# Routing order fixed by hand and low weights last in three-part products, in a hybrid S5, SSD and PEER encoder layer

## The chip, the cores and the metric

The kernel runs on one core of one Trainium2 chip. The metric is the device time of one execution in microseconds. The engines are called PE (TensorE, matmuls), DVE (VectorE), ACT (ScalarE), POOL (GpSimd) and SP (SyncE, which here issues DMAs). PEld is PE's loading of weights.

## The reference

One layer on 512 tokens of width 1024: RMS norm, one input projection, a bidirectional S5 scan, a bidirectional SSD (a convolution and chunked state space), an output projection, and a PEER feed-forward, with residuals around both halves. All is float32; the kernel does its large products in three parts, with each operand split into a high and a low half. What matters here is the feed-forward:

```
q = (x2 @ w_q) as 8 heads x 2 sides x 128
scores = q . sub_keys               # 128 keys a side
s, i = top 16 of each side          # per token, head, side
cand = s[0][:, None] + s[1][None]   # 256 sums, top 16 of these
gate = softmax(best 16);  expert = i0 * 128 + i1   # 16384 experts
y = sum_over_experts gate * gelu(x2 . u[expert]) * v[expert]
```

## The kernel before

The layer is one instruction stream per engine. The order within each stream is set by a scheduler that models costs and follows priorities; the kernel's text gives the dependences. The front (norms, projections, S5, SSD) fills the first 670 us; the feed-forward then has these parts.

*Scores* (`route_scores`): 16 products with `w_q`, 16 small products with the sub-keys, and top16 on DVE by repeated MAX8, FIND_INDEX8 and MATCH_REPLACE8 (`top16`).

*Pick* (`route_pick(t)`, one for each of four tiles of 128 tokens): DVE adds the candidates (`cand`, L954), takes the top 16 per head, turns positions into index pairs (`ge`, `oha`, `ohm`, `ij`, L986 to L998) and normalizes the gates (Exp on ACT, L966; L1003 on DVE). For t of 1 to 3, PE transposes `ij` (L1016, two) and the gates (L1018), and ACT copies the latter (`kS`, L1020).

*Gathered* (`gathered`): token tile 0 is done by indirect DMAs that POOL issues (L1130), with the products on DVE. It needs only the pick of t = 0.

*Gates* (`gates(t)`, t of 1 to 3): 16 pairs of onehots each. DVE makes three tiles a pair (L1035, L1040, L1044), ACT four slices (L1039), PE eight matmuls (L1058, two groups of four), ACT copies to `stg` (L1060), and SP writes `stg` to `G_d` in DRAM (L1062). So the gate of every expert and token stands in `G_d`.

*Dense* (`up(i)` and `dense`): token tiles 1 to 3 are computed against all 128 blocks i of 128 experts. `up(i)` loads a tile of u (`wload`: `w_raw` by DMA, cast to `w_hi` on ACT, `w_lo` as the difference, on POOL for i under NF = 34 and on DVE after), makes 24 matmuls into `hid` (`mm3`, 8 steps of three) and applies Gelu into F (34 buffers). `hid` has two buffers, `w_hi` and `w_lo` two, `w_raw` three. Then for each i, `dense` loads v, multiplies F by its slice of G (L1101; a load G8 serves eight i and reads all of `G_d`), splits the product into Wh and Wl, and accumulates 18 matmuls into six banks (L1113 to L1115); afterwards `up(i + 34)`.

So `up(0)` to `up(33)` need no routing and are what PE can do while the routing runs on DVE; the accumulation needs all 24 writes of `G_d`. The scheduler decides between which tiles of `up` the transposes and gate pairs stand.

Of the kernel before, what the change touches and what calls it, by code (L numbers as in the profile page):

```python
# [9 lines left out]

F32 = mybir.dt.float32
F32R = mybir.dt.float32r
BF16 = mybir.dt.bfloat16
# [2 lines left out]
AF = mybir.ActivationFunctionType  # L16
# [72 lines left out]
class Kernel:  # L89
# [45 lines left out]
    def wload(self, src, k, m, name="w", lo_eng=None):  # L135

        nc = self.nc
        raw = self.wp.tile([128, k, m], F32, name="w_raw", tag="w_raw", bufs=3)
        nc.sync.dma_start(raw, src)
        hi = self.wp.tile([128, k, m], F32R, name="w_hi", tag="w_hi", bufs=2)  # L140
        lo = self.wp.tile([128, k, m], F32R, name="w_lo", tag="w_lo", bufs=2)
        nc.scalar.copy(hi, raw)  # L142
        (lo_eng or nc.vector).tensor_sub(lo, raw, hi.bitcast(F32))  # L143
        return hi, lo

    def mm3(self, ps, ahi, alo, bhi, blo, nk, start=True, stop=True):

        mm = self.nc.tensor.matmul
        for k in range(nk):
            mm(ps, ahi(k), bhi(k), start=start and k == 0, stop=False)  # L150
            mm(ps, ahi(k), blo(k), start=False, stop=False)  # L151
            mm(ps, alo(k), bhi(k), start=False, stop=stop and k == nk - 1)  # L152

    def split(self, hi, lo, src, lo_eng=None):
        self.nc.scalar.copy(hi, src)  # L155
# [789 lines left out]
    def route_pick(self, t):  # L945

        nc, pp = self.nc, self.rp
        V, A, T = nc.vector, nc.scalar, nc.tensor
        sv = self.ts[:, t].rearrange("p (h s) k -> p h s k", s=2)
        cand = pp.tile([128, 8, 50], F32, name="cand", bufs=1)  # L950
        off = 0
        for a in range(8):
            n = 16 // (a + 1)
            V.tensor_add(cand[:, :, off:off + n], sv[:, :, 1, 0:n], sv[:, :, 0, a:a + 1].to_broadcast([128, 8, n]))  # L954
            off += n
        V.tensor_add(cand[:, :, off:off + 8], sv[:, :, 0, 8:16], sv[:, :, 1, 0:1].to_broadcast([128, 8, 8]))
        yield

        best = pp.tile([128, 16, 8], F32, name="best", bufs=1)
        pos = pp.tile([128, 16, 8], U32, name="pos", bufs=1)  # L960
        for h in range(8):
            s2 = pp.tile([128, 50], F32, name="cand2", bufs=2)
            self.top16(best[:, :, h], pos[:, :, h], cand[:, h], s2)
        gt = pp.tile([128, 16, 8], F32, name="gt", bufs=1)
        V.tensor_sub(gt, best, best[:, 0:1, :].to_broadcast([128, 16, 8]))
        A.activation(gt, gt, AF.Exp)  # L966
        yield
        bt = lambda n, tag, m=16: pp.tile([128, m, 16, 8], BF16, name=n, tag=tag, bufs=1)
        posb = pp.tile([128, 16, 8], BF16, name="posb", bufs=1)
        V.tensor_copy(posb, pos)  # L970
        idx = pp.tile([128, 2, 16, 8], BF16, name="idxb", bufs=1)
        for sd in range(2):
            V.tensor_copy(idx[:, sd].rearrange("p a h -> p h a"),
                          self.ti[:, t].rearrange("p (h s) a -> p s h a", s=2)[:, sd])
        ij = pp.tile([128, 2, 16, 8], BF16 if t else F32, name="ij", bufs=1)
        st = pp.tile([128, 16, 8], BF16, name="stb", bufs=1)
        over_a = lambda x: x[:, None].to_broadcast([128, 16, 16, 8])
        over_k = lambda x: x[:, :, None, :].to_broadcast([128, 16, 16, 8])

        def total(x, out):  # L980
            for n in (8, 4, 2):
                V.tensor_add(x[:, 0:n], x[:, 0:n], x[:, n:2 * n])  # L982
            V.tensor_add(out, x[:, 0], x[:, 1])

        ge = bt("ge", "dec", 17)
        V.memset(ge[:, 16], 0.0)  # L986
        V.tensor_tensor(ge[:, 0:16], over_a(posb), over_k(self.first), OP.is_ge)
        oh = bt("oha", "oha")
        V.tensor_sub(oh, ge[:, 0:16], ge[:, 1:17])
        m = bt("ohm", "dec")  # L990
        V.tensor_mul(m, oh, over_k(idx[:, 0]))
        total(m, ij[:, 0])
        V.tensor_mul(m, oh, over_k(self.first))  # L993
        total(m, st)
        yield
        V.tensor_sub(st, posb, st)
        V.tensor_tensor(oh, over_a(st), over_k(self.count), OP.is_equal)  # L997
        V.tensor_mul(m, oh, over_k(idx[:, 1]))  # L998
        total(m, ij[:, 1])
        sm = pp.tile([128, 8], F32, name="gsum", bufs=1)  # L1000
        V.tensor_reduce(sm, gt.rearrange("p k h -> p h k"), axis=AX.X, op=OP.add)
        V.reciprocal(sm, sm)
        V.tensor_mul(gt, gt, sm[:, None, :].to_broadcast([128, 16, 8]))  # L1003
        gt = gt.rearrange("p k h -> p (k h)")
        ij = ij.rearrange("p s k h -> p s (k h)")
        if t == 0:
            self.idx0 = self.hp.tile([128, 128], I32, name="idx0")
            self.gt0 = self.hp.tile([128, 128], F32, name="gt0")
            V.scalar_tensor_tensor(self.idx0, ij[:, 0], 128.0, ij[:, 1], op0=OP.mult, op1=OP.add)
            V.tensor_copy(self.gt0, gt)  # L1010
            return

        kG = self.psm.tile([128, 512], F32, name="kT", tag="mm", bufs=2)
        kT = kG.bitcast(BF16)
        for i in range(2):
            T.transpose(kT[:, i * 128:(i + 1) * 128], ij[:, i], self.identb)  # L1016
        kG = kG[:, 128:256]
        T.transpose(kG, gt, self.ident)  # L1018
        kS = pp.tile([128, 128], F32, name="kS", bufs=2)
        A.copy(kS, kG)  # L1020
        self.kT[t] = kT, kG, kS
        yield

# [40 lines left out]
    def up(self, i):  # L1064

        nc = self.nc
        uh, ul = self.wload(self.I["ut"][i], 8, 128, lo_eng=nc.gpsimd if i < NF else nc.vector)
        ps = self.phid.tile([128, 384], F32, name="hid", bufs=2)
        self.mm3(ps, lambda k: uh[:, k, :], lambda k: ul[:, k, :],
                 lambda k: self.x2h[:, k, 128:512], lambda k: self.x2l[:, k, 128:512], 8)  # L1070
        f = self.fpool.tile([128, 24, 16], F32, name="F", bufs=NF)
        nc.scalar.activation(f.rearrange("p b t -> p (b t)"), ps, AF.Gelu)
        self.F[i] = f
# [47 lines left out]
    def gathered(self):  # L1121

        nc, I, gp = self.nc, self.I, self.gp
        V, A = nc.vector, nc.scalar
        hid = gp.tile([128, 128], F32, name="hid0")
        act = gp.tile([128, 128], F32, name="act0")

        def fetch(tab, k):
            r = gp.tile([128, 1024], F32, name="rowg", bufs=4)
            nc.gpsimd.indirect_dma_start(out=r, out_offset=None, in_=tab,  # L1130
                                         in_offset=bass.IndirectOffsetOnAxis(ap=self.idx0[:, k:k + 1], axis=0))
            return r

        todo = [(p, k) for h in range(8) for p in (0, 1) for k in range(16 * h, 16 * h + 16)]
        ahead = []
        for n, (p, k) in enumerate(todo):
            while len(ahead) < 3 and n + len(ahead) < len(todo):
                pp, kk = todo[n + len(ahead)]
                ahead.append(fetch(I["v"] if pp else I["u"], kk))
            r = ahead.pop(0)  # L1140
            if p == 0:
                d = V.scalar_tensor_tensor(r, r, 1.0, self.xn0, op0=OP.mult, op1=OP.mult,  # L1142
                                           accum_out=hid[:, k:k + 1])
                self.tc.keep_in_program_order(d)
                if k % 16 == 15:
                    ks = slice(k - 15, k + 1)
                    A.activation(act[:, ks], hid[:, ks], AF.Gelu)
                    V.tensor_mul(act[:, ks], act[:, ks], self.gt0[:, ks])
            elif k == 0:
                V.tensor_scalar(self.acc0, r, act[:, k:k + 1], None, op0=OP.mult)  # L1150
            else:
                d = V.scalar_tensor_tensor(self.acc0, r, act[:, k:k + 1], self.acc0, op0=OP.mult, op1=OP.add)  # L1152
                self.tc.keep_in_program_order(d)
            yield
# [20 lines left out]
    def whole(self, last="out"):  # L1175
        nc, tc, I = self.nc, self.tc, self.I
        with ExitStack() as ctx:
# [5 lines left out]
            with ExitStack() as c2:  # L1183
# [25 lines left out]
                hctx.close()  # L1209
                self.rp = self.rctx.enter_context(tc.tile_pool(name="rp", bufs=1, reuse_waits="tile"))  # L1210
                self.kT = {}
                self.col = self.hp.tile([128, 128], F32, name="col")
                nc.gpsimd.iota(self.col, pattern=[[1, 128]], base=0, channel_multiplier=0,
                               allow_small_or_imprecise_dtypes=True)
# [105 lines left out]
```

## Time and profile before

| | us |
|---|---|
| three timed runs | 1872.22, 1877.84, 1880.70 |
| median | 1877.84 |
| profiled execution | 1881.2 |
| its span | 1879.0 |
| mean granted clock of PE | 0.981 |
| busy: PE, DVE, ACT, POOL | 1796.7, 1427.5, 785.8, 609.4 |

The span is what the profiler saw of the profiled execution. PE is busy for 96% of it. Times in the rows below count from the start of the span. In a timeline row stand the start, the duration, the engine, the line in the kernel, the operation, the tile written and the tiles read, the shape, and in brackets how long the engine idled before it and what released it. Ends of matmuls are modelled, and consecutive ones overlap, so the pace is read from their starts.

### The profile page before, as it was taken

The numbers are of one execution on the slowest core, as the hardware profiler recorded it, in microseconds if no ns is written. First come the engines' busy times: TensorE is split into PE (matmuls) and PEld (weight loads), VectorE is DVE, ScalarE is ACT, GpSimd is POOL, SyncE is SP. The second block draws the span as 40 slices with busy tenths as digits, with TensorE's granted clock in tenths as the row PEclk, the third lists the DMA queues.
The fourth block names the chain that finished last, engine by engine and source line by source line (L and its number), as shares of the span: only waits on it lengthen the run. The fifth ranks groups of instructions, "written<-read, shape, count | busy, mean of one in ns | idle before, by whom it ended". The sixth has DMA issues, their size and how long they took to land.

```text
span 1879.0 us, 26537 instructions
## 1 busy us (share of the span) xinstructions
PE 1796.7 (96%) x9351; PEld 1538.8 (82%) x9351; DVE 1427.5 (76%) x2852; ACT 785.8 (42%) x1419; POOL 609.4 (32%) x485
## 2 busy tenths in 40 slices
PE   7999899999999987998999999999999999999998
PEld 3557677777878887898998999999999999999886
DVE  6999956677646799999579777777777777776676
ACT  4235454555323334786633333333333333333333
POOL 1112114444003344222334433434344343343431
PEclk9999999999999998999999999999999999999999
DMA  4322165453742224554799898988989988886675
GB/s 144 107 66 78 53 191 179 124 169 107 240 160 65 99 82 145 202 191 167 247 347 368 293 320 307 309 288 308 315 271 319 314 292 299 312 277 213 248 264 193
DMA packets 174820, 407.40 MB, mean 217 GB/s; under 512 B 20000, under 2 KB 77088, under 8 KB 171616
## 3 DMA queue, kind: packets, MB, share of 16 engines
q1 hardware_dynamic: 129904, 259.85, 41.3%
q0 software_dynamic: 36864, 134.23, 20.1%
q10 hardware_dynamic: 7920, 11.64, 1.8%
q8 instruction: 73, 1.20, 0.3%
q14 instruction: 59, 0.48, 0.1%
HBM read 367.28 MB, written 37.32 MB: 215 GB/s over the span
## 4 chain that ended last, share of the span: by engine, by line
PE 62%; DVE 6%; issue 1%; ACT 1%; DMA 0%; POOL 0%; DVEq 0%; POOLq 0%; ACTq 0%
PE acc L1114 9%; PE acc L1115 9%; PE acc L1113 9%; PE hid L152 8%; PE hid L150 8%; PE hid L151 8%; PE sm L1058 4%; PE mm L150 2%; PE mm L151 2%; PE mm L152 2%; DVE ohm L982 2%; PE sm L904 1%; DVE cand L954 0%; DVE oha L997 0%; DVE ohm L993 0%
## 5 line engine op out<-in xcount | busy, mean ns | idle before, releaser
L142 ACT CAST w_hi<-w_raw 128x1024 fp32r<-128x1024 f32 (+2 forms) x197 | 198.9, 1011 | 438.2 <-PE hid L151 214.2
L152 PE MATMUL hid<-x2h,w_lo 128*128 128x384 f32 x1024 | 351.0, 343 | 12.7 <-POOL w_lo L143 10.7
L150 PE MATMUL hid<-x2h,w_hi 128*128 128x384 f32 x1024 | 350.5, 342 | 3.2 <-ACT w_hi L142 3.1
L151 PE MATMUL hid<-x2l,w_hi 128*128 128x384 f32 x1024 | 349.8, 342 | 0.0
L143 POOL TENSOR_TENSOR w_lo<-w_raw,w_hi 128x1024 fp32r<-128x1024 f32 (+1 forms) x86 | 198.0, 2303 | 373.9 <-ACT w_hi L142 373.8
L1115 PE MATMUL acc<-vh,Wl 128*128 128x512 f32 x768 | 301.0, 392 | 0.0
L1114 PE MATMUL acc<-vl,Wh 128*128 128x512 f32 x768 | 300.8, 392 | 0.0
L1113 PE MATMUL acc<-vh,Wh 128*128 128x512 f32 x768 | 298.7, 389 | 0.0
L1130 POOL DMA_INDIRECT rowg<-in_u_dram,idx x128 | 193.8, 1514 | 274.4 <-DVE rowg L1142 186.9
L143 DVE TENSOR_TENSOR w_lo<-w_raw,w_hi 128x1024 fp32r<-128x1024 f32 (+1 forms) x111 | 135.1, 1217 | 183.8 <-ACT w_hi L142 183.8
L1130 POOL DMA_INDIRECT rowg<-in_v_dram,idx x128 | 164.6, 1286 | 274.8 <-DVE acc L1152 203.8
L152 PEld LDWEIGHTS hid<-x2h,w_lo 128*128 128x128 f32 x1024 | 196.4, 192 | 14.6 <-POOL w_lo L143 12.3
L150 PEld LDWEIGHTS hid<-x2h,w_hi 128*128 128x128 f32 x1024 | 196.7, 192 | 7.9 <-ACT w_hi L142 4.2
L155 ACT CAST Wh<-F 128x384 fp32r<-128x384 f32 x128 | 65.9, 515 | 320.3 <-PE acc L1114 281.0
L151 PEld LDWEIGHTS hid<-x2l,w_hi 128*128 128x128 f32 x1024 | 196.3, 192 | 3.7
L156 DVE TENSOR_TENSOR vl<-v_raw,vh 128x1024 fp32r<-128x1024 f32 x128 | 156.4, 1222 | 17.7 <-ACT vh L155 16.8
L1115 PEld LDWEIGHTS acc<-vh,Wl 128*128 128x128 f32 x768 | 144.1, 188 | 30.3 <-DVE Wl L156 0.3
L1114 PEld LDWEIGHTS acc<-vl,Wh 128*128 128x128 f32 x768 | 144.1, 188 | 28.7 <-DVE vl L156 0.3
L1113 PEld LDWEIGHTS acc<-vh,Wh 128*128 128x128 f32 x768 | 144.3, 188 | 28.2 <-ACT vh L155 0.4
L1152 DVE SCALAR_TENSOR_TENSOR acc<-rowg,act,acc 128x1024 f32<-128x1024 f32 x127 | 162.4, 1279 | 2.8 <-DMA rowg<-in_v_dram,idx 2.7
L1142 DVE SCALAR_TENSOR_TENSOR rowg<-rowg,xn 128x1024 f32<-128x1024 f32 x128 | 151.9, 1219 | 3.6 <-DMA rowg<-in_u_dram,idx 2.1
L155 ACT CAST vh<-v_raw 128x1024 fp32r<-128x1024 f32 x128 | 134.2, 1048 | 4.7 <-DMA v_raw<-in_v_dram 4.7
(387 smaller groups left out, 3111.6 us busy)
## 6 DMA issues: line engine op xcount, KB each, us to landing
w_raw<-in_ut_dram SPq DMA_DIRECT2D x128, 512.0 KB
v_raw<-in_v_dram SPq DMA_DIRECT2D x128, 512.0 KB
G_d<-stg SPq DMA_DIRECT2D x24, 1024.0 KB
G<-G_d SPq DMA_DIRECT2D x16, 1536.0 KB
w_raw<-in_w_in_dram SPq DMA_DIRECT2D x40, 512.0 KB
RB<-rows_d SPq DMA_DIRECT2D x32, 256.0 KB
w_raw<-in_w_q_dram SPq DMA_DIRECT2D x16, 512.0 KB
E<-rows_d SPq DMA_DIRECT2D x32, 128.0 KB
```

Of the source, the lines that this page charges most:

```text
L142: nc.scalar.copy(hi, raw)
L143: (lo_eng or nc.vector).tensor_sub(lo, raw, hi.bitcast(F32))
L150: mm(ps, ahi(k), bhi(k), start=start and k == 0, stop=False)
L151: mm(ps, ahi(k), blo(k), start=False, stop=False)
L152: mm(ps, alo(k), bhi(k), start=False, stop=stop and k == nk - 1)
L155: self.nc.scalar.copy(hi, src)
L156: (lo_eng or self.nc.vector).tensor_sub(lo, src, hi.bitcast(F32))
L1113: mm(a, wh[:, ts], vh[:, hs], start=k == 0, stop=False)
L1114: mm(a, wh[:, ts], vl[:, hs], start=False, stop=False)
L1115: mm(a, wl[:, ts], vh[:, hs], start=False, stop=k == 127)
L1130: nc.gpsimd.indirect_dma_start(out=r, out_offset=None, in_=tab, in_offset=bass.IndirectOffsetOnAxis(ap=self.idx0[:, k:k + 1], axis=0))
L1152: d = V.scalar_tensor_tensor(self.acc0, r, act[:, k:k + 1], self.acc0, op0=OP.mult, op1=OP.add)
```

## The change

First, `mm3` no longer takes the three parts of a product step by step: for each step it issues high by high and high by low, and after all steps the products with the low weights (`alo`). This holds for every three-part product that goes through `mm3`. Second, a helper `order` adds a dependence that only fixes the order in an engine's stream and brings no semaphore. With it the Exp of pick t goes behind the cast of `up(EXPO[t])`, the transposes of t behind the last matmul of `up(TURN[t])`, the copy `kS` behind the cast of `up(TURN[t] + 1)`, and the first three gathers of u behind `w_lo` of `up(10)` to `up(12)`. The scheduler still orders all else.

```diff
+TURN = {1: 14, 2: 23, 3: 31}
+EXPO = {0: 5, 1: 11, 2: 21, 3: 30}
+FIRST_GATHER = 10
...
-        nc.scalar.copy(hi, raw)
-        (lo_eng or nc.vector).tensor_sub(lo, raw, hi.bitcast(F32))
+        self.cast = nc.scalar.copy(hi, raw)
+        self.low = (lo_eng or nc.vector).tensor_sub(lo, raw, hi.bitcast(F32))
         return hi, lo
+
+    def order(self, ins, front):
+
+        self.tc.add_manual_dep(ins.ins, front.ins.name,
+                               mybir.DependencyInfo(mybir.DependencyClass.NoSync, mybir.DependencyReason.DATA),
+                               reason="order of issue")
...
             mm(ps, ahi(k), bhi(k), start=start and k == 0, stop=False)
             mm(ps, ahi(k), blo(k), start=False, stop=False)
-            mm(ps, alo(k), bhi(k), start=False, stop=stop and k == nk - 1)
+        for k in range(nk):
+            d = mm(ps, alo(k), bhi(k), start=False, stop=stop and k == nk - 1)
+        return d
...
-        A.activation(gt, gt, AF.Exp)
+        self.behind.append((A.activation(gt, gt, AF.Exp), "act", EXPO[t]))
...
-            T.transpose(kT[:, i * 128:(i + 1) * 128], ij[:, i], self.identb)
+            self.behind.append((T.transpose(kT[:, i * 128:(i + 1) * 128], ij[:, i], self.identb), "pe", TURN[t]))
         kG = kG[:, 128:256]
-        T.transpose(kG, gt, self.ident)
+        self.behind.append((T.transpose(kG, gt, self.ident), "pe", TURN[t]))
         kS = pp.tile([128, 128], F32, name="kS", bufs=2)
-        A.copy(kS, kG)
+        self.behind.append((A.copy(kS, kG), "act", TURN[t] + 1))
...
+        for ins, eng, n in self.behind:
+            if n == i:
+                self.order(ins, last if eng == "pe" else cast)
+        self.lows[i] = low
...
+            if tab is I["u"] and k < 3:
+                self.order(d, self.lows[FIRST_GATHER + k])
```

Lines of the routing move down by 12, so L1016 is L1028 after, L1058 is L1070; `mm3`'s L150, L151, L152 are L160, L161, L163. Tiles of `up` are told apart by the number behind `hid`: for i up to 33 it is 7724 + 33 i; i = 34 and 35 are 8891 and 8965.

PE at the transposes of token tile 1 (`kT_6354`) before: `hid_7988` is tile 8 of `up`, `hid_8054` tile 10; the first gate matmuls follow 17 `hid` matmuls after the last row here, still in tile 10.

```order
L150 MATMUL hid_7988<-x2h_4959,w_hi_7984 128x384
L1016 LDWEIGHTS ij_6325
L1016 MATMUL kT_6354<-identb_5060,ij_6325 128x128
L151 MATMUL hid_7988<-x2l_4960,w_hi_7984 128x384
...
L151 MATMUL hid_8054<-x2l_4960,w_hi_8050 128x384
L1016 LDWEIGHTS ij_6325
L1016 MATMUL kT_6354<-identb_5060,ij_6325 128x128
L1018 MATMUL kT_6354<-ident_88,gt_6317 128x128
L152 MATMUL hid_8054<-x2h_4959,w_lo_8051 128x384
L150 MATMUL hid_8054<-x2h_4959,w_hi_8050 128x384
```

In the change the three stand together after the last matmul of tile 14 (`hid_8186`); `hid_8219` and `hid_8252` are tiles 15 and 16, `sm` the first gate pair of token tile 1.

```order
L163 MATMUL hid_8186<-x2h_4959,w_lo_8183 128x384 x8
L1028 LDWEIGHTS ij_6325
L1028 MATMUL kT_6354<-identb_5060,ij_6325 128x128
...
L1030 MATMUL kT_6354<-ident_88,gt_6317 128x128
L160 MATMUL hid_8219<-x2h_4959,w_hi_8215 128x384
...
L163 MATMUL hid_8219<-x2h_4959,w_lo_8216 128x384 x8
L160 MATMUL hid_8252<-x2h_4959,w_hi_8248 128x384
L161 MATMUL hid_8252<-x2l_4960,w_hi_8248 128x384
L160 MATMUL hid_8252<-x2h_4959,w_hi_8248 128x384
L1070 MATMUL sm_6383<-oh1_6369,og_6362 128x128 x4
L1070 MATMUL sm_6389<-oh1_6369,og_6363 128x128 x4
```

The transposes moved by some five tiles, and the first gate pair from inside tile 10 to three matmuls into tile 16.

PE at the last gate pairs before, up to the first accumulation: `hid_8615` is tile 27, `hid_8813` tile 33.

```order
L1058 MATMUL sm_7699<-oh1_7666,og_7660 128x128 x4
L150 MATMUL hid_8615<-x2h_4959,w_hi_8611 128x384
...
L151 MATMUL hid_8615<-x2l_4960,w_hi_8611 128x384
L1058 MATMUL sm_7705<-oh1_7691,og_7684 128x128 x4
L1058 MATMUL sm_7711<-oh1_7691,og_7685 128x128 x4
L152 MATMUL hid_8615<-x2h_4959,w_lo_8612 128x384
...
L152 MATMUL hid_8813<-x2h_4959,w_lo_8810 128x384
L1113 MATMUL acc0_8848<-vh_8858,Wh_8863 128x512
L1114 MATMUL acc0_8848<-vl_8859,Wh_8863 128x512
```

The same place in the change: `hid_8965` is tile 35, and from `sm_7549` to `sm_7711` 16 groups, eight pairs, follow each other.

```order
L1070 MATMUL sm_7530<-oh1_7499,og_7493 128x128 x4
L163 MATMUL hid_8965<-x2h_4959,w_lo_8962 128x384 x8
L1070 MATMUL sm_7549<-oh1_7522,og_7515 128x128 x4
L1070 MATMUL sm_7555<-oh1_7522,og_7516 128x128 x4
...
L1070 MATMUL sm_7705<-oh1_7691,og_7684 128x128 x4
L1070 MATMUL sm_7711<-oh1_7691,og_7685 128x128 x4
L1130 MATMUL acc0_8848<-vh_8858,Wh_8863 128x512
L1131 MATMUL acc0_8848<-vl_8859,Wh_8863 128x512
```

The six and a half tiles that stood between the last gate matmul and the first accumulation now stand ahead of the last eight pairs.

DVE between the last write of `ij` of token tile 1 and its first onehot (`oh2_6360`) before; the names 6754 to 6768 belong to the pick of tile 2.

```order
L983 TENSOR_TENSOR ij_6325<-ohm_6332 128x128
L943 MAX_INDEX pos_6755<-best_6754,cand2_6762 128x8
...
L940 MAX_INDEX pos_6755<-best_6754,cand_6744 128x8
L941 MATCH_REPLACE cand2_6768<-best_6754,cand_6744 128x50
...
L942 MAX best_6754<-cand2_6768 128x8
...
L1035 TENSOR_TENSOR oh2_6360<-col2_5062,kT_6354 128x1024
...
L1040 TENSOR_TENSOR og_6363<-oh2_6360,kT_6354 128x512
L1044 TENSOR_TENSOR oh1_6369<-col_5058,kT_6354 128x1024
```

In the change; `ge_6814`, `oha_6817`, `ohm_6819` and `ij_6812` belong to the pick of tile 2, too.

```order
L995 TENSOR_TENSOR ij_6325<-ohm_6332 128x128
L953 MATCH_REPLACE cand2_6768<-best_6754,cand_6744 128x50
...
L999 TENSOR_TENSOR ge_6814<-posb_6807,first_5064 128x2048
...
L1001 TENSOR_TENSOR oha_6817<-ge_6814 128x2048
...
L1003 TENSOR_TENSOR ohm_6819<-oha_6817,idxb_6809 128x2048
...
L995 TENSOR_TENSOR ij_6812<-ohm_6819 128x128
...
L1005 TENSOR_TENSOR ohm_6819<-oha_6817,first_5064 128x2048
L1047 TENSOR_TENSOR oh2_6360<-col2_5062,kT_6354 128x1024
...
L1052 TENSOR_TENSOR og_6363<-oh2_6360,kT_6354 128x512
L1056 TENSOR_TENSOR oh1_6369<-col_5058,kT_6354 128x1024
```

Before, seven rows of the order stand between the two; in the change 52, with the pick of tile 2 up to its first index.

## Rows read from the trace of the kernel before

**Rows 1.** stretches; busy us (instructions) of PE, PEld, DVE, ACT, POOL; clock, DMA, GB/s

```profile
670.80:946.10 275.30, 245.07 (x1603) 239.17 (x1601) 243.32 (x605) 170.06 (x377) 89.37 (x38) 0.94 0.50 180
946.10:1864.20 918.10, 916.11 (x4535) 822.42 (x4535) 679.08 (x861) 322.23 (x452) 353.35 (x253) 1.00 0.86 295
```

**Rows 2.** waits of PE: engine, line, releaser, us in total, times, longest

```profile
PE kT L1016 <- DVE ij L983: 15.3, 5, 4.5
PE hid L152 <- POOL w_lo L143: 10.7, 5, 4.3
...
PE mm L152 <- DVE w_lo L143: 5.0, 1, 5.0
...
PE hid L150 <- ACT w_hi L142: 3.1, 2, 2.8
...
PE hid L152 <- DVE w_lo L143: 2.0, 1, 2.0
```

**Rows 3.** timeline, PE and DVE before 240 us: start, us, instruction, [idle, releaser]

```profile
237.19 0.80 PE L152 MATMUL mm<-xh,w_lo 128*128 128x512 f32 x1 [4.99 <-DVE w_lo L143]
...
237.47 0.42 DVE L430 TENSOR_TENSOR spimv<-sc,sc 64x252 f32<-64x252 f32 x1
```

**Rows 4.** timeline of PE in `up`, tile starts and after a stall

```profile
676.00 0.33 PE L150 MATMUL hid<-x2h,w_hi 128*128 128x384 f32 x1
...
680.16 0.33 PE L150 MATMUL hid<-x2h,w_hi 128*128 128x384 f32 x1
...
695.51 0.52 PE L151 MATMUL hid<-x2l,w_hi 128*128 128x384 f32 x1
...
695.83 0.52 PE L152 MATMUL hid<-x2h,w_lo 128*128 128x384 f32 x1
```

**Rows 5.** the chain in order of time: start, us, what; a gate pair

```profile
744.02 1.78 PE sm L1058 x16
```

**Rows 6.** timeline of PE, last of the first set of transposes

```profile
737.23 0.23 PE L1016 MATMUL kT<-identb,ij 128*128 128x128 bf16 x1 [2.97 <-DVE ij L983]
```

**Rows 7.** timeline of DVE, top16 rounds, the pick, and one product alone

```profile
685.67 0.20 DVE L941 MATCH_REPLACE8 cand<-best,cand 128x50 f32<-128x50 f32 x1
...
686.48 0.19 DVE L941 MATCH_REPLACE8 cand<-best,cand 128x50 f32<-128x50 f32 x1
...
782.40 1.22 DVE L987 TENSOR_TENSOR ge<-posb,first 128x2048 bf16<-128x2048 bf16 x1
...
783.54 2.49 DVE L954 TENSOR_TENSOR cand<-ts 128x128 f32<-128x128 f32 x1
...
789.25 2.43 DVE L1003 TENSOR_TENSOR gt<-gt,gsum 128x128 f32<-128x128 f32 x1
...
792.38 0.23 DVE L983 TENSOR_TENSOR ij<-ohm 128x128 bf16<-128x128 bf16 x1
...
852.38 0.28 DVE L1003 TENSOR_TENSOR gt<-gt,gsum 128x128 f32<-128x128 f32 x1
```

**Rows 8.** timeline of POOL at 789 us

```profile
789.11 2.42 POOL L143 TENSOR_TENSOR w_lo<-w_raw,w_hi 128x1024 fp32r<-128x1024 f32 x1 [3.23 <-ACT w_hi L142]
```

**Rows 9.** timeline of DVE, two pairs of onehots

```profile
747.26 1.22 DVE L1044 TENSOR_TENSOR oh<-col,kT 128x1024 f32<-128x1024 f32 x1
...
749.78 1.21 DVE L1044 TENSOR_TENSOR oh<-col,kT 128x1024 f32<-128x1024 f32 x1
```

**Rows 10.** timeline, ACT, SP queue, DVE, ACT, PE, from last gate to dense

```profile
914.15 0.58 ACT L1060 COPY stg<-sm 128x512 f32<-128x512 f32 x1 [0.31 <-PE sm L1058]
...
921.37 0.38 SPq L1095 DMA_DIRECT2D G<-G_d  x1
...
931.27 0.56 DVE L1101 TENSOR_TENSOR F<-F,G 128x384 f32<-128x384 f32 x1 [4.02 <-DMA G<-G_d]
...
931.86 0.51 ACT L155 CAST Wh<-F 128x384 fp32r<-128x384 f32 x1 [4.54 <-DVE F L1101]
...
946.10 0.39 PE L1113 MATMUL acc<-vh,Wh 128*128 128x512 f32 x1
```

More of the change, by code (lines that the diff above doesn't have):

```diff
@@ L1068, in up @@
         ps = self.phid.tile([128, 384], F32, name="hid", bufs=2)
-        self.mm3(ps, lambda k: uh[:, k, :], lambda k: ul[:, k, :],
-                 lambda k: self.x2h[:, k, 128:512], lambda k: self.x2l[:, k, 128:512], 8)
+        cast, low = self.cast, self.low
+        last = self.mm3(ps, lambda k: uh[:, k, :], lambda k: ul[:, k, :],
+                        lambda k: self.x2h[:, k, 128:512], lambda k: self.x2l[:, k, 128:512], 8)
+        for ins, eng, n in self.behind:
+            if n == i:
+                self.order(ins, last if eng == "pe" else cast)
+        self.lows[i] = low
         f = self.fpool.tile([128, 24, 16], F32, name="F", bufs=NF)
@@ L1129, in fetch @@
             r = gp.tile([128, 1024], F32, name="rowg", bufs=4)
-            nc.gpsimd.indirect_dma_start(out=r, out_offset=None, in_=tab,
-                                         in_offset=bass.IndirectOffsetOnAxis(ap=self.idx0[:, k:k + 1], axis=0))
+            d = nc.gpsimd.indirect_dma_start(out=r, out_offset=None, in_=tab,
+                                             in_offset=bass.IndirectOffsetOnAxis(ap=self.idx0[:, k:k + 1], axis=0))
+            if tab is I["u"] and k < 3:
+                self.order(d, self.lows[FIRST_GATHER + k])
             return r
@@ L1211, in whole @@
                 self.kT = {}
+                self.behind, self.lows = [], {}
                 self.col = self.hp.tile([128, 128], F32, name="col")
```

## Prediction

> **What bounds the kernel now.** I read the stages first. From 946.10 us, where the dense part starts, TensorE (PE) is busy 916.11 of 918.10 us; in the routing stretch, 670.80 to 946.10, only 245.07 of 275.30, at a mean granted clock of 0.94 [rows 1]. The reader should see that the change, which adds no arithmetic, can gain little outside the routing and the part before it.
>
> Then the list of PE's waits [rows 2]: five waits for the pick's indices (15.3 us), five for low weights from POOL (10.7), one of 5.0 for low weights from DVE, two of 3.1 together for cast weights, one of 2.0 for DVE's low weights. The 5.0 stands at 237.19, before the routing [rows 3].
>
> Next, what the routing would take with no wait. Tiles of `up` start 4.16 us apart (676.00, 680.16), 34 tiles are 141.4 [rows 4]. A gate pair (eight matmuls, 16 records) takes 1.78 [rows 5]; three token tiles of 16 pairs are 48, 85.4. The last score job and three sets of transposes add some 1.9. Sum 228.7; the stretch takes 275.3, so **46.6 us** is wait and lower clock. About 30 is idle PE (275.30 less 245.07). The rest is mostly the matmuls after a stall: at 695 they follow each other by 0.32 instead of 0.17 us [rows 4]; over the 9 to 15 matmuls that run so, a restart costs 1.3 to 2.2 us. I count 2 for each long wait.
>
> **The change, part by part.** Two edits: low-weight matmuls last in each product, and an order fixed by hand. What is fixed holds in the instruction streams, as the rows of the order show, so "it does not do what it says" is no case here. The sum goes against the profiled execution (1881.2 us; span 1879.0); the median shown is 1877.84, 3.4 lower, and I carry the difference over to it.
>
> *Front (0 to 670.8).* The wait of 5.0 is for low weights that stand fourth in the row; now 16 high-weight matmuls of that tile, and of the next, come ahead. At the tile pace they are worth more than 5.0, so the wait goes, with its slow restart: -6. What is late next is the chain of S5's scan on DVE, whose last piece (237.47 to 237.89) was ready just as PE came out of this wait [rows 3]; if that or another wait takes over, 0. Since the scheduler also reweaves this part, I keep -7 to +3.
>
> *Waits for weights in the routing.* Low weights now have 16 matmuls (2.8 us) more, and the Exp and the first gathers are put where they no longer stand ahead of a cast or a `w_lo`. The 10.7 and 3.1 are costed at 0; the wait for low weights could only come back if `w_lo` were over 2.8 us late again, as the longest was (4.3 of the 10.7) behind a gather on POOL.
>
> *First transposes.* Before, PE met them inside tiles 8 and 10 and stood 2.97 at 737.23, the last of several stalls [rows 6]. Now PE runs tiles 0 to 14 without a stall and meets all three after tile 14, at 670.8 + 0.9 + 15 x 4.16 = 734.1. DVE delivered `ij` at 737.2; with nothing else changed PE waits 3.1. But more `w_lo` run on POOL meanwhile (one per tile, up to tile 16 instead of 11), and they hold DVE up: the product at L1003 takes 0.28 us alone (852.38) but 2.43 at 789.25, exactly while a `w_lo` of 2.42 runs on POOL from 789.11; `cand` at 783.54 shows the same, 2.49 [rows 7, 8]. Seven such rows lie between 692.49 and 734.52, at eight starts of `w_lo`. Each costs some 2.15. With none more, the wait is 3; with six more 16. I take 9, about three more, since some of the new `w_lo` fall on MAX8 and FIND_INDEX8 rows, which show no such stretch. Plus 2 for the restart.
>
> The Trainium skill ("SBUF — State Buffer", section "Who interferes with whom") says that a DVE instruction with two SBUF inputs and a GpSimd instruction that reads SBUF exclude each other, and the later one waits for the whole of the other. The rows at 789 agree, 2.43 against 0.28. By that rule alone every further `w_lo` that meets such an instruction costs its full length, which is the 16 above.
>
> *First gate of t=1.* Now the whole first half of the next pick stands on DVE between `ij` and the first onehot. Its price: six rounds of top16 at 0.81 (685.67 to 686.48), 4.9; the section from 782.40 to 792.38, 9.98, less two stretches of 2.1 that come from POOL, 5.8; one more 2048-wide product, 1.1: 11.8 [rows 7]. The onehots of a pair add 2.5 (747.26 to 749.78) [rows 9]. So the first gate matmul comes 14.3 after `ij`; PE has 0.4 of transposes, tile 15 and three matmuls, 5.1, as cover. Wait 9.2, one stretched instruction more makes 11.3: I take 10 (9 to 13.5), plus 2.
>
> *Gates of t=1 and 2.* Before, a pair with five `hid` matmuls is 1.78 + 0.87 = 2.65 on PE, and DVE's 2.5 hides under it. Now the second half of the next pick is woven into DVE's onehots: about 6 us in place of about 2.5, so DVE paces: +3 each, 6 (0 to 9). The first gate of t=2 has five tiles, 20 us, ahead of it, and DVE some 15 of work: 2 for a stretched instruction or two. The transposes of t=2 and 3 come late enough for DVE to be done: 0 instead of what they held of the 15.3.
>
> *Last gates.* Eight pairs stand bare at the end, with no `hid` between: DVE's 2.5 against 1.78, 8 x 0.72 = 5.8 (0 to 9).
>
> *From the last gate to the first accumulation.* Before, 6.5 tiles (about 27 us of PE work) stood behind the last gate, and this chain ran beneath them: last copy to `stg` 914.15, load of G issued 921.37, product with G on DVE 931.27, cast of Wh ends 932.37; 18.2 in all, while the first `acc` came at 946.10 [rows 10]. Now the accumulation follows the last pair directly, so the cover is gone and the chain is bare. Fewer `w_raw` loads share the queues with G: 17 (13 to 21), plus 2. This is the largest term, and the price of having spent those tiles earlier.
>
> Sum of waits after: 9 + 2 + 10 + 2 + 6 + 2 + 5.8 + 17 + 2 = **55.8** against 46.6: +9.2 in the routing. Front -6. Dense part: the wait of 2.0 and its restart go, -2.5 (0 to -3); all else there is unchanged, since PE has no other idle time. Net **+0.7**: 1881.9 for such a profile, 1878.5 against the median. So what the early tiles lose in stalls, the end pays back.
>
> **Rivals.**
> 1. *Faster: DVE is not held up more than before.* Waits 3 + 2 for the transposes, 9 + 2 for the first gate, 2 for both gate sets, 2 for t=2, 2 for the bare pairs, 13 + 2 for the chain: 37, that is -9.6; front and dense -9. Net -18.6, 1859. For it: MAX8 rows are not stretched, and POOL's extra starts may fall on those; G's load has fewer neighbours. Against it: seven of eight starts did meet a two-input instruction.
> 2. *Slower: POOL holds DVE at full price on the whole path to the gates.* Six more stretched instructions than I count (6 x 2.15 = 13) before and inside the gates of t=1 and 2, with a restart, 15: net about +15, 1893. It decides from four more than counted (8.7 / 2.15). For it: rows 7 and 8. Against: once PE stands, no tile is finished, and `w_lo` has two buffers, so POOL soon stands too.
> 3. *The front is rewoven without gain.* S5's scan, not the weights, sets the pace there, and the -6 becomes 0 or +3: 1885 to 1888. For it: the wait ended just as the scan was ready; against: PE is busy nearly throughout the stretches behind it.
>
> **Chances.** Forecast 0.46, rival 1 0.27, rival 2 0.19, rival 3 0.08. A measurement of this kernel tells about 0.5% (9.4 us) from no change. Faster by more: rival 1 and a share of 0.03 of the third's cases in which the weave of the front gains; slower: rival 2 and 0.03 of the third, in which it loses more; together 0.30, 0.48, 0.22. The forecast's own range is 1868 to 1888; for eight in ten it reaches to rival 1 (1859) and past rival 2 (1893): 1859 to 1895.
>
> **What would show it.** In the changed kernel's profile: no wait of a `hid` low-weight matmul for POOL, and none at 237; one wait of about 9 of the transposes for `ij`, the others near none; the first gate matmul standing about 10 for a onehot; pairs of t=1 and 2 at about 2.85 us; PE idle for about 17 ahead of the first `acc`, released by Wh or the product with G. I am wrong if that last gap is under 10, if the transposes' wait is over 15 (rival 2) or under 4 and the gates' at PE's pace (rival 1), or if the front ends as late as before.

## The result and the profile after

Over 14 runs each, the changed kernel takes 1889.11 us (median, 1881.69 to 1896.28), the kernel before 1878.28 (1872.22 to 1881.60). The ratio is 1.006, 95% interval 1.0048 to 1.0072: 0.6% slower. The forecast was 1878 within 1859 to 1895. The time lies in the range, on its slow side, 11 us from the likeliest case, and just beyond the 0.5% that the forecast called no change; it gave a time that much slower a chance of 0.22.

The profiled execution took 1888.06 us, span 1885.2, which is 6.2 over the span of before. By stage, from the first tile of `up` and the first accumulation of both traces:

| stage | before | after | difference | forecast |
|---|---|---|---|---|
| to the first tile of `up` | 670.78 | 673.02 | +2.2 | -6 |
| to the first accumulation, less 8.3 for the two more tiles of `up` ahead of it | 275.32 | 281.2 | +5.9 | +9.2 |
| to the last accumulation, plus 8.3 | 923.91 | 921.9 | -2.0 | -2.5 |

The three stages of the changed kernel, columns as in [rows 1]:

```profile
0.00:673.00 673.00, 627.67 (x3190) 471.71 (x3191) 497.68 (x1374) 291.51 (x579) 170.53 (x192) 0.97 0.39 126
673.00:962.50 289.50, 246.86 (x1650) 243.08 (x1648) 257.40 (x611) 176.54 (x379) 97.80 (x46) 0.94 0.53 189
962.50:1870.00 907.50, 907.44 (x4485) 813.71 (x4486) 679.89 (x851) 329.82 (x450) 326.87 (x244) 1.00 0.85 293
```

PE's longest waits in it that answer to [rows 2]:

```profile
PE sm L1070 <- DVE oh L1056: 17.4, 8, 7.5
PE acc L1130 <- ACT Wh L167: 14.6, 1, 14.6
...
PE sm L682 <- ACT sq L677: 6.5, 3, 4.2
PE hid L160 <- ACT F L1089: 4.6, 1, 4.6
...
PE kT L1028 <- DVE ij L995: 3.6, 1, 3.6
PE sm L689 <- POOL rsg L686: 3.2, 3, 2.3
...
PE sm L564 <- ACT BN L560: 2.8, 1, 2.8
...
PE kT L1030 <- DVE gt L1015: 1.7, 1, 1.7
```

No wait of a `hid` matmul for low weights is left, and the 5.0 at 237 is gone. In their place stand two waits of the gates and the accumulation, and in the front longer waits for ACT and POOL (`sq` 6.5, before 3.5; `rsg` 3.2, before 1.3). PE's timeline in the routing, with the wait and its releaser in brackets:

```profile
724.77 0.52 PE L160 MATMUL hid<-x2h,w_hi 128*128 128x384 f32 x1 [4.59 <-ACT F L1089]
...
746.92 0.29 PE L1028 MATMUL kT<-identb,ij 128*128 128x128 bf16 x1 [3.61 <-DVE ij L995]
...
748.95 0.48 PE L1030 MATMUL kT<-ident,gt 128*128 128x128 f32 x1 [1.74 <-DVE gt L1015]
...
763.02 0.55 PE L1070 MATMUL sm<-oh,og 128*128 128x128 f32 x1 [7.53 <-DVE oh L1056]
...
936.42 2.02 PE L1070 MATMUL sm<-oh,og 128*128 128x128 f32 x16 [1.44 <-DVE oh L1056]
...
939.89 2.02 PE L1070 MATMUL sm<-oh,og 128*128 128x128 f32 x16 [1.45 <-DVE oh L1056]
...
962.53 0.80 PE L1130 MATMUL acc<-vh,Wh 128*128 128x512 f32 x1 [14.63 <-ACT Wh L167]
```

The reader should see, in order: an unforeseen wait for Gelu's F; two waits at the transposes (before, [rows 6]); the wait for the first onehot; two of the bare last pairs, 3.47 apart; and the gap before the first accumulation. The first of them comes from the fixed order itself. ACT shows the Exp of token tile 1 (L978), now behind the cast of `up(11)`, and ahead of a Gelu that frees a `hid` buffer for PE; the Exp's input from DVE is late, and all that stands behind it on ACT waits with it:

```profile
722.60 0.31 ACT L978 ACTIVATE gt<-gt 128x128 f32<-128x128 f32 x1 [5.54 <-DVE gt L977]
...
724.22 0.49 ACT L1089 ACTIVATE F<-hid 128x384 f32<-128x384 f32 x1
```

DVE shows what stretches a bare pair, a gathered product of token tile 0 between two onehots [rows 9]:

```profile
935.06 1.21 DVE L1056 TENSOR_TENSOR oh<-col,kT 128x1024 f32<-128x1024 f32 x1
...
936.79 1.21 DVE L1161 SCALAR_TENSOR_TENSOR rowg<-rowg,xn 128x1024 f32<-128x1024 f32 x1
...
938.53 1.21 DVE L1056 TENSOR_TENSOR oh<-col,kT 128x1024 f32<-128x1024 f32 x1
```

From the last copy to `stg` over the load of G to the product, as in [rows 10]: 961.38 - 947.94 = 13.4, where it was 17.1.

```profile
947.94 0.58 ACT L1072 COPY stg<-sm 128x512 f32<-128x512 f32 x1 [0.31 <-PE sm L1070]
...
953.51 0.37 SPq L1112 DMA_DIRECT2D G<-G_d  x1
...
961.38 0.56 DVE L1118 TENSOR_TENSOR F<-F,G 128x384 f32<-128x384 f32 x1 [4.35 <-DMA G<-G_d]
```

### The profile page after: what moved, and what is told of

The parts are those of the page before. It is cut to its first block, busy times and chain, and to the rows that moved or that the text cites. A ratio compares the mean times of both kernels' runs of the same rounds, so it can differ in the third digit from the quotient of the medians.

```text
span 1885.2 us, 26554 instructions
## 1 busy us (share of the span) xinstructions
PE 1788.5 (95%) x9351; PEld 1533.5 (81%) x9351; DVE 1444.1 (77%) x2852; ACT 802.0 (43%) x1419; POOL 596.8 (32%) x485
## 4 chain that ended last, share of the span: by engine, by line
PE 62%; DVE 7%; issue 1%; DMA 1%; POOL 0%; ACT 0%; DVEq 0%; POOLq 0%; SPq 0%; ACTq 0%
PE acc L1131 9%; PE acc L1132 9%; PE acc L1130 9%; PE hid L161 8%; PE hid L160 8%; PE hid L163 8%; PE sm L1070 4%; PE mm L160 2%; PE mm L161 1%; PE mm L163 1%; DVE ohm L994 1%; PE sm L916 1%; DVE oh L1056 1%; DVE cand L966 1%; DMA G<-G_d 0%
## 5 line engine op out<-in xcount | busy, mean ns | idle before, releaser
L160 PE MATMUL hid<-x2h,w_hi 128*128 128x384 f32 x1024 | 346.6, 338 | 4.6 <-ACT F L1089 4.6
L161 PE MATMUL hid<-x2l,w_hi 128*128 128x384 f32 x1024 | 348.1, 340 | 0.0
L1130 PE MATMUL acc<-vh,Wh 128*128 128x512 f32 x768 | 299.6, 391 | 14.7 <-ACT Wh L167 14.6
L147 POOL TENSOR_TENSOR w_lo<-w_raw,w_hi 128x1024 fp32r<-128x1024 f32 (+1 forms) x86 | 202.9, 2359 | 317.9 <-PE mm L163 114.8
L1147 POOL DMA_INDIRECT rowg<-in_u_dram,idx x128 | 174.6, 1364 | 335.2 <-DVE rowg L1161 254.5
L163 PE MATMUL hid<-x2h,w_lo 128*128 128x384 f32 x1024 | 201.5, 335 | 0.0
L160 PEld LDWEIGHTS hid<-x2h,w_hi 128*128 128x128 f32 x1024 | 194.4, 190 | 8.5 <-ACT F L1089 4.9
L161 PEld LDWEIGHTS hid<-x2l,w_hi 128*128 128x128 f32 x1024 | 194.2, 190 | 3.6
L163 PEld LDWEIGHTS hid<-x2h,w_lo 128*128 128x128 f32 x1024 | 178.6, 188 | 0.0
L1131 PEld LDWEIGHTS acc<-vl,Wh 128*128 128x128 f32 x768 | 144.7, 188 | 28.5
```

What stands on the lines that cost most here:

```text
L147: self.low = (lo_eng or nc.vector).tensor_sub(lo, raw, hi.bitcast(F32))
L163: d = mm(ps, alo(k), bhi(k), start=False, stop=stop and k == nk - 1)
L1130: mm(a, wh[:, ts], vh[:, hs], start=k == 0, stop=False)
L1131: mm(a, wh[:, ts], vl[:, hs], start=False, stop=False)
L1147: d = nc.gpsimd.indirect_dma_start(out=r, out_offset=None, in_=tab, in_offset=bass.IndirectOffsetOnAxis(ap=self.idx0[:, k:k + 1], axis=0))
```

## The experiments

Ratios are to the kernel before, of runs beside it on the same chip, with 95% intervals. Each edit is made on the changed kernel; "no order" means that `order` is never called, and `last` is an argument of `mm3` that puts the low weights last.

### The parts of the change, one at a time

**front_only**: no order, and `up` as before.

```diff
+        last = self.mm3(..., 8, last=False)   # in up
-                self.order(ins, ...)
```

> Low weights last in every product of the front, but not in the tiles of `up`, and no order fixed by hand: PE's order up to the first tile of `up` is that of the changed kernel, behind it nearly that of the kernel before. Theory (the front is the step that failed): the first tile of `up` starts at about 673 us as in the changed kernel (673.02) instead of 670.78, with the 5.0 wait at 237 gone and the SSD's waits for ACT, POOL and DVE (sq, rsg, BN, xw) longer; time +2 us on before, ratio about 1.001. Rival (the front gains 6 as predicted, and the single profile of the changed kernel was a late one): first tile at 665, ratio 0.997.

Ratio 1.003 [1.0012, 1.0049], 1883.37 us. The theory's direction holds; the loss is larger than it said, 5.6 us (2.3 to 9.2 by the interval). Its one profiled execution (1880.83) is 2.5 under its median and starts `up` at 671.44, 0.7 later than before, so the profile hardly shows where the loss falls.

**up_and_order**: the front as before, the rest as changed.

```diff
+    def mm3(..., last=False):
+        last = self.mm3(..., 8, last=True)   # in up
```

> The fixed order, and low weights last in the tiles of `up` alone: PE's order in the front is that of the kernel before, in the routing that of the changed kernel. Theory (front +2, routing +6, dense -2 make the loss): first tile at 670.8, 36 tiles to the first accumulation in about 289.5 us, total about 1882 to 1884, ratio 1.002 to 1.003, faster than the changed kernel by 2 to 6 us. Rival (the loss is all in the routing): as slow as the changed kernel, ratio 1.006.

Ratio 1.0028 [1.0012, 1.0044]. The theory holds: with front_only it gives 1.0058, the 1.006 of the whole. PE's two longest waits are those of the changed kernel:

```profile
PE sm L1072 <- DVE oh L1058: 19.7, 9, 8.6
PE acc L1132 <- ACT Wh L169: 14.5, 1, 14.5
```

**up_only**: the same, without the order.

```diff
-                self.order(ins, last if eng == "pe" else cast)
...
-                self.order(d, self.lows[FIRST_GATHER + k])
```

> Low weights last in the tiles of `up` alone, no order fixed by hand. Theory (in the routing the time is set by the pick on DVE, and PE's stalls for weights only take the place of stalls for indices): the 10.7 us of waits for POOL's low weights shrink, the waits for `ij` grow by nearly as much, time within 4 us of before, ratio 0.998 to 1.002. Rival (each stall of PE removed is a gain): ratio 0.994, some 11 us faster with the restarts.

Ratio 0.9971 [0.9957, 0.9984], 1871.41 us, between the two. No wait for POOL's low weights is left; the waits for `ij` grew from 15.3 to 28.5:

```profile
PE kT L1030 <- DVE ij L997: 28.5, 6, 13.6
...
PE mm L163 <- DVE w_lo L147: 5.0, 1, 5.0
```

**order_only**: the order, and no product with low weights last.

```diff
-        for k in range(nk):
-            d = mm(ps, alo(k), bhi(k), ...)
+            d = mm(ps, alo(k), bhi(k), ...)   # in the loop ahead
```

> The fixed order alone, with the three parts of each product in the order of before. Theory (the loss in the routing comes from the order: the first gate waits for the next pick, the last pairs are bare and so is the chain to the first accumulation): 36 tiles to the first accumulation in 286 to 292 us, ratio 1.002 to 1.006. Rival (low weights last make the loss, and the order by itself gains, since the gathers and the Exp no longer stand ahead of weights): ratio under 0.998.

Ratio 1.0063 [1.0047, 1.0080], just above the 1.002 to 1.006 of the theory; 36 tiles take 288.8 us, as it said. Against up_only and up_and_order: the order costs 0.6% whether or not the low weights are last, and low weights last in `up` give 0.3%.

**front_win**: as front_only, but with `last` for the input projection's products alone.

```diff
+                self.mm3(..., k, last=xh is self.win_in)
```

> Low weights last in the products of the input projection only; the other products of the front, and `up`, in the order of before, no order fixed by hand. Theory (the loss of the front is in the weave of the input projection with S5 and SSD): as slow as front_only, ratio 1.002 to 1.004. Rival (it comes from the later products, w_glu to w_q): ratio 1.000 or less.

Ratio 1.0030 [1.0018, 1.0042], as front_only: the order of the input projection's products, which alone is changed here, makes the loss. From the first tile of `up` on, PE, DVE, ACT and POOL have the order of before, instruction by instruction. Nor is it the granted clock of PE, on average 0.982 here and before. That the loss falls in the weave with S5 and SSD is likely but not shown: the one profiled execution is the fastest of the eleven, 5.4 under their median, and starts `up` at 669.97, 0.8 earlier than before. What it does show is a longer wait for `sq` in SSD, 6.9 (3.0 to 5.5 in the nine traces that have the front in the order of before):

```profile
PE sm L684 <- ACT sq L679: 6.9, 3, 4.5
```

**up_two**: up_only, and `last` in two calls of `mm3` in the front.

```diff
+                self.calls += 1
+                self.mm3(..., k, last=self.calls in (8, 9))
```

> up_only, and low weights last in just two tiles of the front's input projection, the one whose low weights PE waits 5.0 us for at 237 and the one behind it; PE's order elsewhere is that of up_only. Theory (the wait can be had back, and it is the reweaving of the many other products of the front that loses it): the wait at 237 is gone, the first tile of `up` starts 4 to 6 us earlier than in up_only, ratio to before 0.994 to 0.995. Rival (the engines that feed SSD set the pace behind the wait, whatever the order): the other waits of PE between 250 and 330 us grow by as much, ratio as up_only, 0.997.

Ratio 0.9933 [0.9917, 0.9949], 1865.45 us: 6 under up_only, `up` starts 4.9 earlier (664.60 against 669.49). The theory holds, and the rival in part. Two places of SSD, its first `xcT` transposes and its first `rsg`, show it. PE's timeline before:

```profile
258.24 0.27 PE L547 MATMUL sm<-ident,xcT 128*128 128x128 f32 x1
...
325.87 0.58 PE L677 MATMUL sm<-ident,rsg 128*128 128x128 f32 x1 [0.56 <-POOL rsg L674]
```

In the changed kernel:

```profile
250.13 0.27 PE L559 MATMUL sm<-ident,xcT 128*128 128x128 f32 x1
...
329.19 0.58 PE L689 MATMUL sm<-ident,rsg 128*128 128x128 f32 x1 [0.26 <-POOL rsg L686]
```

In front_only:

```profile
253.31 0.27 PE L561 MATMUL sm<-ident,xcT 128*128 128x128 f32 x1
...
328.21 0.58 PE L691 MATMUL sm<-ident,rsg 128*128 128x128 f32 x1 [0.26 <-POOL rsg L688]
```

In up_two:

```profile
247.85 0.27 PE L562 MATMUL sm<-ident,xcT 128*128 128x128 f32 x1
...
321.32 0.58 PE L692 MATMUL sm<-ident,rsg 128*128 128x128 f32 x1
```

At the first place all three lead, by 8.1, 4.9 and 10.4 us. At the second the changed kernel is 3.3 behind, front_only 2.3 behind, up_two still 4.6 ahead. The nine traces with the front's order of before reach the second place between 323.4 and 327.4, and the first tile of `up` between 668.4 and 671.5, so a step of 2 or 3 us is near the spread; but low weights last throughout the input projection lie above it at the second place (front_win too, 328.73), and up_two and two_dve below it at both (321.32 and 319.25; 664.60 and 665.89). So a lead won at 237 is half lost on the way through SSD even where the order stays, and wholly lost where all products are rewoven.

### The terms of the routing

**no_wlo**: up_and_order, in which tiles 4 to 18 of `up` have no low weights made.

```diff
+        if not low:              # 4 <= i <= 18
+            return hi, hi
```

> up_and_order without the low weights of tiles 4 to 18 of `up`: POOL makes none there, and the products with low weights take the high ones instead, so that PE has the same work. Theory (each low-weight subtraction on POOL holds up a DVE instruction with two SBUF inputs by some 2.1 us): the last index of token tile 1 is ready some 18 to 25 us earlier, PE meets the transposes after tile 14 without a wait (735 to 738), the first gate follows with a wait under 4 instead of 8.6, and no row of L1017 is over 0.4 us. Rival (the stretched rows have another cause): the transposes wait for `ij` until 741 or later, as in up_and_order.

One execution, 1862.59 us, in a kernel that leaves out work the result needs. No row of L1017's product is long any more. DVE's last `ij` of token tile 1 and that product in no_wlo:

```profile
722.22 0.20 DVE L1000 TENSOR_TENSOR ij<-ohm 128x128 bf16<-128x128 bf16 x1
...
725.52 0.27 DVE L1020 TENSOR_TENSOR gt<-gt,gsum 128x128 f32<-128x128 f32 x1
```

and in up_and_order:

```profile
742.27 0.21 DVE L997 TENSOR_TENSOR ij<-ohm 128x128 bf16<-128x128 bf16 x1
...
743.13 1.71 DVE L1017 TENSOR_TENSOR gt<-gt,gsum 128x128 f32<-128x128 f32 x1
```

From the first tile of `up` (671.79 and 670.78) `ij` comes after 50.4 instead of 71.5, 21.1 earlier, with 12 fewer subtractions on POOL (3 instead of 15): 1.8 each. The same 269 instructions run on DVE up to that `ij` in both kernels, so the difference is POOL's. The stretch from the first tile of `up` to the first accumulation shrinks by 23.4 (266.6 against 289.9), although PE has the same matmuls. PE meets the transposes without a wait, and the first gate starts 5.0 after the first of them:

```profile
735.24 0.23 PE L1033 MATMUL kT<-identb,ij 128*128 128x128 bf16 x1
...
740.20 0.35 PE L1075 MATMUL sm<-oh,og 128*128 128x128 f32 x1
```

**wlo_hi2**: up_only, 13 subtractions on DVE.

```diff
+        with self.tc.high_priority(100000 if fast else 0):
+            self.low = (lo_eng or nc.vector).tensor_sub(...)
+  fast = 4 <= i <= 10 or 15 <= i <= 17 or 22 <= i <= 24   # on nc.vector
```

> up_only with the low weights of 13 tiles of `up`, those that fall on the picks (4 to 10, 15 to 17, 22 to 24), made on DVE (1.22 us each) instead of POOL. Theory (a subtraction on POOL costs a pick some 2.1 us of DVE's time, more than DVE needs to do it): the routing gets 13 x 0.6, some 5 to 8 us, shorter, first gate of token tile 1 at 62 to 65 us after the first tile instead of 67.8, ratio to before 0.993 to 0.996. Rival (POOL's work on low weights is for the most part free to DVE): the picks get 13 x 1.22, some 16 us, longer, ratio 1.003 or more.

Ratio 0.9945 [0.9925, 0.9964], 4 us under up_only in the medians, though the intervals of the two overlap: the time came as the theory said, but not the way. The first gate follows the first tile after 68.4, not 62 to 65. Up to the last `ij` of token tile 1, seven subtractions on DVE (8.5 us) and five fewer on POOL (6 instead of 11) leave that `ij` where it was, 64.3 against 64.0 after the first tile: some 1.6 us saved for each that left POOL. That bears out the price and speaks against the rival, but it buys PE tiles and not an earlier gate: 35 instead of 34 tiles lie ahead of the first accumulation, in 267.3 against 268.2 us, and PE's waits for `ij` fell from 28.5 to 20.1:

```profile
PE kT L1031 <- DVE ij L998: 20.1, 6, 4.4
```

**turnless**: up_and_order, with the Exp and the first gathers in their fixed places, transposes and `kS` free.

```diff
-        self.behind.append((T.transpose(kG, gt, self.ident), "pe", TURN[t]))
+        T.transpose(kG, gt, self.ident)   # so the other two, and kS
```

> Low weights last in the tiles of `up` alone; of the fixed order only the places of the Exp and of the first gathers, while the transposes and the copy `kS` stand where the scheduler puts them. Theory (the loss of about 11 us between up_only and up_and_order comes from the turns of the transposes): about as fast as up_only, ratio 0.996 to 0.999. Rival (the places of Exp and gathers make the loss, as PE's wait of 4.6 for Gelu's F behind an Exp suggests): ratio 1.001 or more.

Ratio 1.0042 [1.0029, 1.0055]: the theory, that the turns alone lose, falls. With the transposes free, the Exp of token tile 3, fixed behind the cast of `up(30)`, holds DVE for 22.4:

```profile
DVE gsum L1015 <- ACT gt L980: 22.4, 1, 22.4
```

What the places of the first gathers cost by themselves stays open.

**turn3_28**: up_and_order with an earlier turn for token tile 3.

```diff
-TURN = {1: 14, 2: 23, 3: 31}
+TURN = {1: 14, 2: 23, 3: 28}
```

> up_and_order with the transposes of token tile 3 after tile 28 of `up` instead of 31. Theory (in the fixed order DVE stands about 10 us for the copy `kS` of tile 3, while PE has tiles to do, and these tiles are then missing behind the last gate): the last gate comes about 10 us earlier, two tiles stand between it and the first accumulation, the bare gap there falls from 14.5 to 6 or less; time 8 to 12 us under up_and_order, ratio to before 0.996 to 0.999. Rival (the pick of tile 3 on DVE is late as well, so the wait only moves to the transposes): within 3 us of up_and_order, ratio 1.002.

Ratio 1.0002 [0.9989, 1.0014], 5 under up_and_order, half of what the theory said. The longest wait of DVE in the routing of up_and_order is gone:

```profile
DVE oh L1049 <- ACT kS L1034: 10.5, 1, 10.5
```

The last gate comes 258.4 us after the first tile of `up` instead of 275.2, and two tiles stand behind it, yet PE's gap before the first accumulation is still 14.6. The load of G now shares the DMA engines with gathers and a load of u, and takes 16.1 from issue to product instead of 7.8 in up_and_order; of the 5.72 MB moved in that time, 2.85 are gathers:

```profile
934.99 0.38 SPq L1114 DMA_DIRECT2D G<-G_d  x1
...
951.08 0.56 DVE L1120 TENSOR_TENSOR F<-F,G 128x384 f32<-128x384 f32 x1 [5.74 <-DMA G<-G_d]
```

**rowg_late**: up_and_order, gathered products behind the last onehot.

```diff
+                if k < 16:
+                    self.order(d, self.onehot)   # the last L1058
```

> up_and_order with DVE's first gathered products put behind the last onehot. Theory (the last pairs take 3.47 us each, not 2.5, since DVE has a gathered product of 1.2 in each): the bare pairs run at 2.4 to 2.6, the last gate comes 7 to 9 us earlier, time 6 to 8 us under up_and_order, ratio to before 0.998 to 1.000. Rival (the pairs are bound by ACT's slices and copies, not by these products): pairs at 3.2 or more, time within 2 us of up_and_order.

Ratio 1.0039 [1.0025, 1.0053]: no faster than up_and_order. The bare pairs do run 2.52 apart (931.37 to 933.89) and the last gate comes 8.4 earlier from the first tile, as the theory said of its cause; but the products, which wait for their gathers, now stand ahead of the product with G on DVE, and PE's gap grew from 14.5 to 24.6:

```profile
942.86 1.23 DVE L1163 SCALAR_TENSOR_TENSOR rowg<-rowg,xn 128x1024 f32<-128x1024 f32 x1 [4.53 <-DMA rowg<-in_u_dram,idx]
...
951.97 1.23 DVE L1163 SCALAR_TENSOR_TENSOR rowg<-rowg,xn 128x1024 f32<-128x1024 f32 x1 [1.98 <-DMA rowg<-in_u_dram,idx]
...
959.34 0.56 DVE L1120 TENSOR_TENSOR F<-F,G 128x384 f32<-128x384 f32 x1 [5.00 <-DMA G<-G_d]
...
960.50 0.80 PE L1132 MATMUL acc<-vh,Wh 128*128 128x512 f32 x1 [24.58 <-ACT Wh L169]
```

**two_dve**: up_two and wlo_hi2 together.

> up_two and wlo_hi2 together: low weights last in the tiles of `up` and in two tiles of the front, the low weights of 13 tiles on DVE, no order fixed by hand. Theory (the two gains lie in different stretches and add): the first tile of `up` some 5 us earlier than in wlo_hi2, the routing as there; ratio to before 0.990 to 0.992, some 1860 to 1862 us, the fastest of all. Rival (they overlap): 0.993 or more, as up_two alone.

Ratio 0.9909 [0.9888, 0.9929], 1859.72 us: the first tile of `up` starts 5.6 earlier than in wlo_hi2 (665.89 against 671.53), the routing takes 263.3 against 267.3, and the ratio is what the two gains over up_only give together, 0.991. Its interval overlaps that of up_two, so the share of the 13 subtractions, some 0.25% here as in wlo_hi2, rests on both kernels together. This is the fastest kernel of the study, 0.9% under the kernel before.

## Why the prediction was right and where it failed

*As a whole: in the range, in part by luck.* The range reached to 1895 for rival 2, POOL at full price; what the sum missed was the front, rival 3, the least likely one. Against the profile the terms sum to +0.7, and +6.2 was measured: the front came out 8.2 worse than its term, the routing 3.3 better.

*Front: failed.* The prediction said "so the wait goes, with its slow restart: -6". The wait went; the stage did not gain. The front ends 2.2 later than before in the changed kernel's profile, which the prediction had named as a sign of being wrong, and front_only's runs measure +5.6 us in place of -6. The step that failed is the account of one wait as a gain of the stage, while the same edit reordered every product of the input projection. The price of the wait itself was right: up_two, which edits two of these products, gains 6 to 7. The prediction had this case as its third rival, at 0.08 and +3 at the most; what was argued against it, that PE is busy behind the wait, says nothing of another order: the wait for `sq` is 5.7 to 6.9 in the three traces with low weights last throughout the input projection, 3.0 to 5.5 in the nine with the order of before. Open is where the typical executions of front_only and front_win lose 5.6 us, since their profiled ones start `up` 0.7 later and 0.8 earlier than before; no profile of a long one was taken.

*Waits for weights: right.* None is left in `up`. But 13.8 us of waits gone are not 13.8 gained: removing them without the order (up_only) gives 5.5 us, and the waits for `ij` grow by 13.2. The places of the Exp, which the prediction took as free, were not: that is the 4.6 below.

*Transposes: 9 + 2; measured 5.4 (3.61 and 1.74), and 4.6 not foreseen.* The stretched rows are as charged, ten over 1.9 us in up_and_order against seven before [rows 7, 8], and no_wlo shows their cause: with 12 subtractions fewer there is no wait here at all. The 4.6 is the wait for Gelu's F behind the Exp; PE reached the transposes that much later, so DVE could go on, and with it the term is 10.0.

*First gate: 10; measured 7.53. Gates of t = 1 and 2: 3 each; measured 3.2 and 4.4* (763.02 to 808.73 and 833.19 to 878.95, before 42.5 and 41.4). *First gate of t = 2: 2; measured 2.1.*

*Bare pairs: 5.8; measured 8.5 of waits in seven pairs* (0.7 of it for ACT's copy to `stg`), within the bounds. Not DVE's onehots alone, 2.5, but a gathered product with each; rowg_late gives 2.5 without them.

*Bare chain: 17; measured 14.6.* The bound of 13 to 21 held, and the reason given too: fewer transfers beside the load of G. turn3_28 shows the other side of it, 16.1 for the load with gathers beside it.

*Sum of the routing: +9.2 forecast, +5.9 in the profile, and +0.28% (5.3 us) by up_and_order, which has the dense part's -2 in it.* But for the 4.6, the waits are where the prediction put them, most within 3 us. That the order loses (0.6%) and low weights last in `up` gain (0.3%) the sum held together and did not tell apart.

*Dense: -2.5 forecast, -2.0 measured.*

Of the rivals, the second's mechanism (POOL holds DVE) is real, and no_wlo shows it worth 21 us up to the last `ij` of token tile 1; but most of that stood in the kernel before as well (eleven subtractions ahead of that `ij`, sixteen in the changed kernel), and the extra 13 us did not come. The third decided: its bounds of 0 to +3 hold the profile's +2.2, not the runs' +5.6.

## What to carry to other kernels

A wait seen on the busiest engine is worth its length only if nothing else is moved to remove it: edit the two products that wait, not the helper that all share. An order fixed by hand on one engine also fixes when the next may start, so count the waits of both, here PE's 4.6 behind an Exp on ACT, DVE's 10.5 for `kS` and PE's 14.6 at the end. Work put into a gap must be followed to what stands behind it in the same queue, as the gathered products before the product with G.

## What the runs showed of the hardware

- A subtraction on POOL cost DVE 1.8 us on average on the way to the last `ij` of token tile 1 (12 of them, 21.1 us, between no_wlo and up_and_order), three quarters of its own 2.4; with 12 gone, no row of DVE on that way is over 1.9 us, where there were ten. These rows agree with the rule of the Trainium skill that the prediction named ("SBUF — State Buffer", section "Who interferes with whom").
- Not only products with two inputs are stretched: a cast of DVE with one input takes 0.46 us, and 2.58 while POOL makes low weights (up_only's timeline, DVE and POOL):

```profile
776.32 0.46 DVE L987 CAST idxb<-ti 128x128 bf16<-128x128 uint32 x1
...
776.58 2.58 DVE L987 CAST idxb<-ti 128x128 bf16<-128x128 uint32 x1
...
776.29 2.56 POOL L147 TENSOR_TENSOR w_lo<-w_raw,w_hi 128x1024 fp32r<-128x1024 f32 x1 [10.70 <-ACT stg L1074]
```

- The load of G, 1.5 MB, took 7.9 us from issue to the product in the changed kernel, with loads of v and no gathers beside it, 9.9 before, with loads of u and v, and 16.1 in turn3_28, where gathers moved half of the bytes.
